# A new hand order for the attention part: row maxima product by product, transposes of v, mixer splits and a table load in other places

## The chip, the cores and the metric

One core of one Trainium2 chip runs the whole block as one program. The metric is device time in microseconds, lower is better; the kernel before took 1288.55 us (median of three runs, 1285.93 to 1289.34). The profile is one execution, taken by the hardware profiler. Five engines have an instruction queue each: TensorE (PE; its weight loads are listed as PEld), VectorE (DVE), ScalarE (ACT), GpSimd (POOL) and SyncE (SP, which here issues every DMA). Each queue is served in order.

## The reference, cut to what matters

A block of a streaming encoder over 16 meta tokens and 1024 frames, width 1024, all in float32. The mixer has four retention heads and eight forgetting-attention heads of width 64; the attention is

```
logits = einsum('bqhd,bkhd->bhqk', q, k) * dh**-0.5 + c_q - c_k      # c: running sum of log f
p      = softmax(where(causal & valid, logits, -1e30))
o_f    = einsum('bhqk,bkhd->bqhd', p, v)
h      = h + concat(o_r, o_f) @ w_out
h      = h + conv_ffn(rms_norm(h))
```

A final norm follows. The change touches only the order in which the attention and what lies around it are issued.

## The kernel before

Products that need float32 precision are made of three matmuls: each operand is split into a rounded high part and a low part (`split`, line 116: ACT writes the high part, another engine subtracts), and high by high, high by low and low by high are summed in a PSUM bank.

After the retention heads comes the attention part, some 185 to 560 us of the span. Its order on TensorE, DVE, ACT and POOL is written out by hand (`tc.manual_schedule`): what the program emits first runs first on each engine. Two streams are woven together.

The dense stream is the generator `dense()` (line 632). It goes through units of 96 matmuls, each giving one 128-wide slice of a projection: fq, fk, fv (queries, keys, values of a pair of heads) and rg (a retention gate); the last one is fv3. Each unit has four chunks (24 matmuls of some 256 columns), each evicted by DVE (L672, L674) from the two banks psD. It yields 120 budget units a matmul, and `run(upto)` draws from it until the budget `done` reaches `upto`. A unit is thus U = 11,520. Side work is put in a list `late` and popped after so many matmuls ("ticks"): `v_tiles` (line 602) transposes a chunk of v into the one bank psT (L606), from which ACT and DVE write high and low parts (L611, L612); in fv3, also splits of mixer tiles 0 to 3 (`split_m`, line 872). What is left at the end of fv3 is flushed with a yield of 400 each. Then `fill` (line 884) does the output projection's first six of eight mixer tiles for six output slices (L894, 160 units a matmul of 342 columns); before the tiles 4 and 5 are used for the first time, they are split. They are loaded while fv3 runs.

The attention stream goes through eight heads with 13 steps each (`units`; a step is at most 512 columns of logits in one psS bank, and there are three of these). A step t draws half of its dense share, issues its logits (`part_s`: L787, mask L791; ACT exponentiates, L797, and rounds, L799), the low part of the step before (`part_d`, L805), other work by the step's number in its head (`at`), the other half of the dense share (`run(want)`), and the value products of three steps ago (`part_v`, L824). The budget `GOAL` gives a head some 21,900 units, a step 1,685, half a step 842, which is seven matmuls.

The maxima of a head's logits are needed before its first step, so they are built a head ahead. `max_step(h, j)` (line 721) takes the queries of row tile j against all keys up to it, 512 columns to a product: one product for j = 0 to 3, two for 4 to 7, three for 8, 15 in all. Each product takes a psS bank (L730, its last one with a mask, L732), and DVE reduces it (L733). `max_end` combines them (L738 to L741). `max_rows` (line 744) transposes the result in psT (L747), ACT copies it (L749), and SP writes it to DRAM (`md`, L750) and reads it back into two rows of `qB` (L752, L753), which the head's logits use. Today row tiles go to steps by

```
SPLIT = (4, 4, 5, 5, 6, 7, 8, 8, 9)     # row tile j -> step of the head before
```

so the steps 4 to 9 issue 2, 2, 2, 2, 4 and 3 products, all at once; `max_end` comes at step 9, `max_rows` at step 10 ahead of the second half of the dense share. Head 0's products are woven into the unit fv0 by lines of their own, a row tile after every 768 units. `prep_k` and `prep_q` (lines 697, 712) make a head's operands: two ACT copies, two DVE subtractions, DMAs for the second copies. `norm2` (step 10) applies the softmax sums.

When all is done, the rest of the output projection starts (`rest_mm` L1069; DVE adds the residual, L1081; ACT squares it, L1093 and L1104). Behind its first slice a dummy square root (`warm`, L1419) makes ACT load the table of that function, which later norms use.

Of the kernel before, what the change touches and what calls it, by code (L numbers as in the profile page):

```python
# [12 lines left out]
AF = mybir.ActivationFunctionType  # L13
# [4 lines left out]
P = 128  # L18
NM = 16
NF = 1024  # L20
NT = NM + NF
# [60 lines left out]
def tile_hymba_block(ctx, tc, xt, xn, wrv0, wrv1, wft, wout, wup, wdn, small, cst, rope, dtab, out):  # L82
# [549 lines left out]
    def dense():  # L632
        late, c = [], 0

        def add(*x):
            nonlocal c
            if not late:
                c = 0
            late.extend(x)

        def tick():
            nonlocal c
            c += 1
            if late and c >= late[0][0]:
                late.pop(0)[1]()
                c = 0

        for u, nm in enumerate(units_w):
            kind, i_ = nm[:2], int(nm[2])
            if kind == "wo":  # L650
                break
            w_dma(u + 1)
            chunks = CX_Q if kind in ("fq", "rg") else CX_T
            t0 = Q0 if kind in ("fq", "rg") else 0
            if kind in ("fq", "fk"):
                st = fq.tile([P, NT], F32, tag=kind, name=kind)
                (qst if kind == "fq" else kst)[i_] = st
            else:
                st = stage("vst" if kind == "fv" else "gate")
                st = st[:, :NQ] if kind == "rg" else st  # L660
            for ci, (a, n) in enumerate(chunks):
                ps = bank(pj)
                for k in range(KT):
                    w_h, w_l = (t[:, k % 4, :] for t in wts[u][k // 4])
                    for i, (w_, e) in enumerate(((w_h, 0), (w_h, 1), (w_l, 0))):
                        pe.matmul(ps[:, :n], lhsT=w_, rhs=X(e, k, t0 + a, n),  # L666
                                  start=(k == 0 and i == 0), stop=(k == KT - 1 and i == 2))
                        yield 120
                        tick()
                rbs = rb[:, t0 + a:t0 + a + n]  # L670
                if kind == "fq":
                    dve.scalar_tensor_tensor(st[:, t0 + a:t0 + a + n], ps[:, :n], 0.125, rbs, op0=ALU.mult, op1=ALU.mult)  # L672
                else:
                    dve.tensor_tensor(st[:, a:a + n], ps[:, :n], rbs, op=ALU.mult)  # L674
                if ci == 1:
                    w_split(u + 1)
                if kind == "fv":
                    add((16, lambda st=st, i_=i_, g=VT[ci]: v_tiles(st, i_, *g)))
                if nm == "fv3":
                    for k in (2 * ci, 2 * ci + 1):  # L680
                        mt[k] = xbuf(ci, f"m{k}")[:, :2 * NQ].rearrange("p (i n) -> p i n", i=2)
                        if k < NA:
                            load_m(k, mt[k])
                    if ci in (1, 2):
                        add(*[(8, lambda k=k: split_m(k)) for k in (2 * ci - 2, 2 * ci - 1)])
            if kind == "rg":
                add(*[(14, g) for g in gate_tail(i_, st)])
        for _, g in late:
            yield 400
            g()  # L690
        wb_done[0] = True
        yield from fill(units_w.index("wo0"))
# [25 lines left out]
        dve.tensor_tensor(qB[s][h_, c], qst[p][h_, c], f(q1[s])[h_, c], op=ALU.subtract)  # L718
        dup[0] = sp.dma_start(f(q1[s])[o_, c], f(q1[s])[h_, c])

    def max_step(h, j):
        s = h % 2
        t0, R = KTILES[j]
        q_ = Q0 if j == 0 else 0
        w = min(NT, P * j + P)
        for ci, a in enumerate(range(0, w, 512)):
            n = min(512, w - a)
            last = a + n == w
            ps = bank(pS)
            pe.matmul(ps[:R - q_, :n], lhsT=qm[s][:, t0 + q_:t0 + R], rhs=kB[s][:, a:a + n], start=True, stop=not last)  # L730
            if last:
                pe.matmul(ps[:R - q_, n - R:n], lhsT=msk[:, q_:R], rhs=idr[:, :R], start=False, stop=True)  # L732
            dve.tensor_reduce(mxs[s][:R - q_, j, ci:ci + 1], ps[:R - q_, :n], axis=mybir.AxisListType.X, op=ALU.max)  # L733
# [150 lines left out]
    def fill(u0):  # L884
        pss = {}

        def part(d, ci, ks, first, stop):
            if first:
                pss[ci] = bank(pj)
            ps, (a, n) = pss[ci], CH_Q[ci]  # L890
            for k in ks:
                w_h, w_l = (t[:, k % 4, :] for t in wts[u0 + d][k // 4])
                for i, (w_, hl) in enumerate(((w_h, 0), (w_h, 1), (w_l, 0))):
                    pe.matmul(ps[:, :n], lhsT=w_, rhs=mt[k][:, hl, a:a + n],  # L894
                              start=(first and k == ks[0] and i == 0), stop=(stop and k == ks[-1] and i == 2))
                    yield 160
            if stop:
                dve.tensor_tensor(hst[d][:, a:a + n], ps[:, :n], hst[d][:, a:a + n], op=ALU.add)

        h_load(0)  # L900
        w_dma(u0 + 1)
        for d in range(EARLY):
            h_load(d + 1)
            if d == 0:
                yield from part(d, 0, range(4), True, False)
                yield from part(d, 1, range(4), True, False)
                split_m(4)
                split_m(5)
                yield from part(d, 0, range(4, 6), False, True)
                yield from part(d, 1, range(4, 6), False, True)  # L910
            else:
                yield from part(d, 0, range(6), True, True)
                w_split(u0 + d + 1)
                w_dma(u0 + d + 2)
                yield from part(d, 1, range(6), True, True)
            if d == 0:
                w_split(u0 + d + 1)
                w_dma(u0 + d + 2)
            yield from part(d, 2, range(6), True, True)
            sp.dma_start(hres[d], hst[d])  # L920
        w_split(u0 + EARLY + 1)
# [6 lines left out]
    done = [0]  # L928
# [9 lines left out]
    V = U  # L938
# [5 lines left out]
        GOAL[h] = max(GOAL[h], u * U + 1)  # L944
    for h, u in ((2, 7), (4, 11)):
        GOAL[h] = min(GOAL[h], u * U)
    SPLIT = (4, 4, 5, 5, 6, 7, 8, 8, 9)
    with tc.manual_schedule(engines=ENG):
        for s_ in range(2):
            rs_ = fp.tile([P, NQ], F32, tag="o", name="rss", bufs=2)  # L950
# [8 lines left out]
            max_step(0, j)  # L959
        run(2 * U + V * 14 // 15)  # L960
        m2 = max_end(0)
        prep_k(1)
        prep_q(1)
        run(2 * U + V + 1 + U // 8)
        max_rows(0, m2)
        scale_rows(1, lambda n: fp.tile([P, NQ], F32, tag="o", name=n, bufs=2))
        run(GOAL[0])
        for h in range(2, 4):
# [1 line left out]
        for t in range(len(units) + LAG):  # L970
            h, at = divmod(t, NU)
            if h < 7:
                want = GOAL[h] + (GOAL[h + 1] - GOAL[h]) * (at + 1) // NU
            else:
                want = GOAL[7] + (END - GOAL[7]) * (t - 7 * NU + 1) // (NU + LAG)
            run((done[0] + want) // 2)
            if h == 6 and at == 4:
                fqs.close()
                wA[0] = mk(fqs, "wA", side="right")
            if h == 6 and at == 4:  # L980
                m7 += [mt[7][:, 0, :], mt[7][:, 1, :]]
            if h == 6 and at == 12:
                load_m(6, mt[6])
                w6r = mk(wb, "w6r")
                for d in range(4):
                    wo_raw[d] = w6r.tile([P, (KT - NA) * P], F32, name=f"wo_raw{d}")
                    sp.dma_start(wo_raw[d], wout[d][:, NA * P:])
            if h == 7 and at == 4:
                split_m(6)
            if t < len(units):  # L990
                part_s(t)
            if 0 <= t - 1 < len(units):
                part_d(t - 1)
            if 0 < h and at == 6:
                norm1(h - 1)
            if 0 < h and at == 10:
                norm2(h - 1)
            if t < len(units):
                if h < 7:
                    if at == 0 and h > 0:  # L1000
                        prep_q(h + 1)
                    if at == 1 and h > 0:
                        prep_k(h + 1)
                    for j in range(9):
                        if SPLIT[j] == at:
                            max_step(h + 1, j)
                    if at == SPLIT[8]:
                        m2 = max_end(h + 1)
                    if at == SPLIT[8] + 1:
                        max_rows(h + 1, m2)  # L1010
            run(want)
            if t - LAG >= 0:
                part_v(t - LAG)
        run(1 << 50)
# [378 lines left out]
    with tc.manual_schedule(engines=ENG):  # L1393
# [20 lines left out]
        for di, d in enumerate(ORD):  # L1414
            r = mm(0, di)
            if di < 4:
                split_w(di + 2)
                if di == 0:
                    act.activation(warm, epsc, AF.Sqrt)  # L1419
            rest_h(0, d, r)  # L1420
            rest_acc(0, rest_sq(0, d), dve if di == 7 else pool)
            if di == 1:
# [486 lines left out]
```

## Time and profile before

| | |
|---|---|
| median of three runs | 1288.55 us (1285.93 to 1289.34) |
| the profiled execution, its own time | 1289.05 us |
| its span, from first to last instruction | 1287.2 us |
| TensorE matmuls busy | 1253.1 us, 97% |
| weight loads | 1189.2 us, 92% |
| DVE | 910.1 us, 71% |
| ACT | 588.8 us, 46% |
| POOL | 348.7 us, 27% |
| mean granted clock of TensorE | 0.991 |

A busy time is the time in which at least one instruction of the engine ran. Weight loads run beside matmuls. In rows of single instructions the columns are start and duration in us, engine, line, operation, tiles (written<-read), shape and count; in brackets the idle time before it and what ended it. A wait names the engine and line that waits, and the one whose signal came last.

### The profile page before, as it was taken

The page shows a single profiled execution, that of the slowest core. Times are in us where ns is not written, and L with a number is a line of the kernel's source. Part 1 is how long each engine was busy: PE and PEld are TensorE (multiplying, and loading weights), DVE is VectorE, ACT ScalarE, POOL GpSimd, SP SyncE. Part 2 cuts the span into 40 slices and gives each one's busy share as a digit, 9 for nine tenths or more (in the row PEclk, how much of TensorE's full clock was granted, in tenths as well). Part 3 has the DMA queues.
Part 4 walks back from the last instruction along what each step waited for, and adds up shares of the span by engine and source line. Part 5 has one row for each costly group of instructions (what it writes and reads, how often), then busy time and mean ns, then how long its engine had stood idle before and what let it go on. Part 6 is the DMA issues. An engine that isn't in the chain of part 4 may idle for free.

```text
span 1287.2 us, 24215 instructions
## 1 busy us (share of the span) xinstructions
PE 1253.1 (97%) x9279; PEld 1189.2 (92%) x9279; DVE 910.1 (71%) x1568; ACT 588.8 (46%) x1174; POOL 348.7 (27%) x294
## 2 busy tenths in 40 slices
PE   8999999999999989999899999999999999999997
PEld 8899999999999989988899999999999998888886
DVE  5776545556665576658987887879889887585664
ACT  7663441456355444445443343333433335544453
POOL 0154244000000000012254554645546450140001
PEclk9999999999999999999999999999999999999998
DMA  8533114213224435364154534537565579866652
GB/s 292 174 88 105 36 51 115 69 43 79 81 62 112 123 108 166 100 222 135 58 192 128 180 118 154 162 114 227 169 215 188 181 231 348 296 212 199 192 167 99
DMA packets 110965, 192.78 MB, mean 150 GB/s; under 512 B 15160, under 2 KB 50312, under 8 KB 110849
## 3 DMA queue, kind: packets, MB, share of 16 engines
q1 hardware_dynamic: 110848, 191.23, 47.0%
q8 instruction: 73, 1.20, 0.4%
q14 instruction: 44, 0.35, 0.1%
HBM read 132.59 MB, written 52.21 MB: 144 GB/s over the span
## 4 chain that ended last, share of the span: by engine, by line
PE 82%; DVE 6%; issue 4%; DMA 3%; ACT 3%; POOL 1%; SPq 0%; POOLq 0%; DVEq 0%; ACTq 0%
PE psb L1232 13%; PE psD L666 12%; PE psc L1232 9%; PE psa L1232 9%; PE psO L824 4%; PE psD L894 4%; PE psb L1388 3%; PE psx L1388 3%; PE psa L1388 3%; PE psc L1388 3%; PE psS L787 3%; PE psj L183 2%; PE psj L185 2%; PE psj L184 2%; PE psS L730 2%
## 5 line engine op out<-in xcount | busy, mean ns | idle before, releaser
L1198 DVE TENSOR_TENSOR d_u<-d_raw,d_u 128x512 fp32r<-128x512 f32 x154 | 110.0, 760 | 53.6 <-ACT d_u L1197 53.4
L1197 ACT CAST d_u<-d_raw 128x512 fp32r<-128x512 f32 x154 | 88.4, 619 | 92.3 <-PE psc L1388 35.3
L666 PE MATMUL psD<-xl,f_hi 128*128 128x256 f32 (+2 forms) x448 | 129.9, 290 | 0.0
L666 PE MATMUL psD<-xh,f_hi 128*128 128x256 f32 (+2 forms) x448 | 128.9, 288 | 0.4 <-DVE fq L672 0.4
L666 PE MATMUL psD<-xh,f_lo 128*128 128x256 f32 (+2 forms) x448 | 128.8, 288 | 0.0
L1193 POOL TENSOR_TENSOR S<-u_raw 128x512 f32<-128x512 f32 x42 | 59.7, 1420 | 203.0 <-DVE unit L1211 169.0
L1232 PE MATMUL psb<-B0T,unit 128*128 128x256 f32 x780 | 104.0, 282 | 1.6 <-DVE unit L1211 0.9
L1232 PE MATMUL psb<-B1T,unit 128*128 128x256 f32 x780 | 103.4, 281 | 1.3 <-ACT B1T L1158 1.2
L797 ACT ACTIVATE pf<-psS 128x272 f32<-128x272 f32 (+4 forms) x112 | 49.7, 451 | 113.8 <-PE psS L787 69.9
L1232 PEld LDWEIGHTS psb<-B0T,unit 128*128 128x128 f32 x780 | 97.2, 189 | 2.2 <-DVE unit L1211 1.4
L1232 PEld LDWEIGHTS psb<-B1T,unit 128*128 128x128 f32 x780 | 97.1, 189 | 1.7 <-ACT B1T L1158 1.5
L666 PEld LDWEIGHTS psD<-xh,f_hi 128*128 128x128 f32 x448 | 85.4, 191 | 0.9 <-DVE fq L672 0.6
L666 PEld LDWEIGHTS psD<-xl,f_hi 128*128 128x128 f32 x448 | 85.2, 190 | 0.4
L666 PEld LDWEIGHTS psD<-xh,f_lo 128*128 128x128 f32 x448 | 85.2, 190 | 0.1
L1211 DVE TENSOR_TENSOR unit<-S,unit 128x512 fp32r<-128x512 f32 x87 | 78.7, 906 | 4.2 <-ACT unit L1207 3.9
L1394 POOL MEMSET on<- 128x128 f32 x1 | 0.2, 204 | 296.5 <-PE psS L791 296.5
L733 DVE TENSOR_REDUCE mx<-psS 128x1 f32<-128x512 f32 (+6 forms) x120 | 59.0, 539 | 30.2 <-PE psS L730 20.9
L1207 ACT CAST unit<-S 128x512 fp32r<-128x512 f32 x87 | 54.1, 622 | 54.1 <-POOL S L1193 53.4
L183 PE MATMUL psj<-rv_hi,xh 128*128 128x256 f32 (+1 forms) x264 | 76.1, 292 | 1.7 <-DVE z L287 1.1
L1271 ACT ACTIVATE ca<-at,sm 128x1024 f32<-128x1024 f32 x22 | 25.3, 1152 | 110.0 <-DVE at L1263 110.0
L184 PE MATMUL psj<-rv_lo,xh 128*128 128x256 f32 (+1 forms) x264 | 75.5, 288 | 0.1
L185 PE MATMUL psj<-rv_hi,xl 128*128 128x256 f32 (+1 forms) x264 | 75.3, 288 | 0.0
(350 smaller groups left out, 3567.1 us busy)
## 6 DMA issues: line engine op xcount, KB each, us to landing
u_raw<-wup SPq DMA_DIRECT2D x44, 512.0 KB
sd<-wdn SPq DMA_DIRECT2D x88, 128.0 KB
uB<-u SPq DMA_DIRECT2D x44, 256.0 KB
wS<-sd SPq DMA_DIRECT2D x88, 128.0 KB
d_raw<-wS SPq DMA_DIRECT2D x44, 256.0 KB
d_raw<-uT SPq DMA_DIRECT2D x44, 256.0 KB
d_raw<-wdn SPq DMA_DIRECT2D x33, 256.0 KB
d_raw<-uB SPq DMA_DIRECT2D x33, 256.0 KB
```

The source lines that it names most:

```text
L183: pe.matmul(ps[:, :w], lhsT=x_h, rhs=w_h[:, c0:c0 + w], start=(k == 0), stop=False)
L184: pe.matmul(ps[:, :w], lhsT=x_h, rhs=w_l[:, c0:c0 + w], start=False, stop=False)
L185: pe.matmul(ps[:, :w], lhsT=x_l, rhs=w_h[:, c0:c0 + w], start=False, stop=(k == KT - 1))
L666: pe.matmul(ps[:, :n], lhsT=w_, rhs=X(e, k, t0 + a, n), start=(k == 0 and i == 0), stop=(k == KT - 1 and i == 2))
L733: dve.tensor_reduce(mxs[s][:R - q_, j, ci:ci + 1], ps[:R - q_, :n], axis=mybir.AxisListType.X, op=ALU.max)
L1193: (eng or pool).tensor_tensor(t, s_[x], s_[y], op=o)
L1197: act.copy(t[:, 0], src)
L1198: eng.tensor_tensor(t[:, 1], src, f(t[:, 0]), op=ALU.subtract)
L1207: act.copy(t[:, 0], srcs[ft][nm])
L1211: dve.tensor_tensor(t[:, 1], srcs[ft][SEQ[i][0]], f(t[:, 0]), op=ALU.subtract)
L1232: pe.matmul(ps[:, :n], lhsT=w[:, wi, k * P:(k + 1) * P], rhs=o[:, hl, k, :], start=(new and j == 0), stop=(j == 11), skip_group_check=not new)
L1388: pe.matmul(ps[:, c:c + n], lhsT=a_[:, wi, j * P:(j + 1) * P], rhs=b_[:, hl, c:c + n], start=(new and m == 0), stop=(kt == KH - 1 and m == ...
```

## The change

The same instructions are issued in another order; none is added or taken away.

- `max_step` can issue one product alone. In the main loop the 15 products go to the steps 4 to 9 as 3, 3, 2, 2, 2 and 3, and between two of a step an equal part of the second half of its dense share is drawn. `max_end` stays at step 9, behind the last product.
- `max_rows` at step 10 comes behind the second half of the dense share instead of ahead of it.
- For head 0, `max_rows` comes at the end of fv0 (2U + V + 1, with V = U), and head 1's `prep_k` and `prep_q` behind it, U/8 later; before, they came right behind `max_end`, and `max_rows` was last.
- The transposes of v are popped after 22 matmuls instead of 16. In fv3 this moves the splits of tiles 0 and 1 by six matmuls, and the third group of transposes to the flush, which has four groups with a yield of 400 instead of three.
- In `fill`, tile 4 is split ahead of the first 12 matmuls, tile 5 ahead of the second 12, instead of both behind the 24.
- The dummy square root comes behind the last exponentials (step index `len(units)`), instead of into the rest of the projection.

```diff
@@ dense
                 if kind == "fv":
-                    add((16, lambda st=st, i_=i_, g=VT[ci]: v_tiles(st, i_, *g)))
+                    add((22, lambda st=st, i_=i_, g=VT[ci]: v_tiles(st, i_, *g)))
@@ max_step
-    def max_step(h, j):
+    def max_step(h, j, only=None):
...
         for ci, a in enumerate(range(0, w, 512)):
+            if only not in (None, ci):
+                continue
@@ fill
             if d == 0:
+                split_m(4)
                 yield from part(d, 0, range(4), True, False)
+                split_m(5)
                 yield from part(d, 1, range(4), True, False)
-                split_m(4)
-                split_m(5)
@@ main loop of the attention part
-    SPLIT = (4, 4, 5, 5, 6, 7, 8, 8, 9)
+    MAXS = [(j, ci) for j in range(9) for ci in range((min(NT, P * j + P) + 511) // 512)]
+    SPLIT = {4: 3, 5: 3, 6: 2, 7: 2, 8: 2, 9: 3}
...
         m2 = max_end(0)
+        run(2 * U + V + 1)
+        max_rows(0, m2)
+        run(2 * U + V + 1 + U // 8)
         prep_k(1)
         prep_q(1)
-        run(2 * U + V + 1 + U // 8)
-        max_rows(0, m2)
...
+            if t == len(units):
+                act.activation(warm, epsc, AF.Sqrt)
...
-                    for j in range(9):
-                        if SPLIT[j] == at:
-                            max_step(h + 1, j)
-                    if at == SPLIT[8]:
+                    if at in SPLIT:
+                        lo = sum(v for k, v in SPLIT.items() if k < at)
+                        n_ = SPLIT[at]
+                        b0_ = done[0]
+                        for x in range(n_):
+                            max_step(h + 1, *MAXS[lo + x])
+                            if x < n_ - 1:
+                                run(b0_ + max(0, want - b0_) * (x + 1) // n_)
+                    if at == 9:
                         m2 = max_end(h + 1)
-                    if at == SPLIT[8] + 1:
-                        max_rows(h + 1, m2)
             run(want)
+            if h < 7 and at == 10:
+                max_rows(h + 1, m2)
@@ rest of the output projection
                 split_w(di + 2)
-                if di == 0:
-                    act.activation(warm, epsc, AF.Sqrt)
```

## The prediction

> **What bounds the kernel now.** I read the page first, then busy times by stretch, then the waits of the weight loader in the attention part, then single instructions in order of time at each place that the change touches.
>
> ```profile
> PE 1253.1 (97%) x9279; PEld 1189.2 (92%) x9279; DVE 910.1 (71%) x1568; ACT 588.8 (46%) x1174; POOL 348.7 (27%) x294
> ```
>
> TensorE is busy 97% of the span. The change takes no matmul away, so all it can gain is time in which TensorE stands. The page hides part of that, because ends of matmuls are modelled; the idle time of the weight loader PEld, and the distance between two matmuls' starts, show it better. By stretch (start:end, length, then busy time of PE, PEld, DVE, ACT and POOL with counts, PE clock, DMA share, GB/s), the first row being the attention part:
>
> ```profile
> 233.00:560.00 327.00, 320.46 (x2475) 308.00 (x2474) 199.86 (x396) 163.03 (x338) 0.20 (x1) 0.99 0.34 98
> ...
> 460.00:464.00 4.00, 3.28 (x21) 2.68 (x19) 3.68 (x9) 1.78 (x5) 0.00 (x0) 1.00 0.46 146
> ...
> 468.00:472.00 4.00, 2.07 (x11) 1.29 (x11) 3.73 (x8) 2.09 (x3) 0.00 (x0) 1.00 0.00 0
> 472.00:476.00 4.00, 4.00 (x17) 3.92 (x18) 2.99 (x5) 1.80 (x5) 0.00 (x0) 0.57 0.17 21
> ```
>
> DVE is at 61% of the part (199.86 of 327) and ACT at 50%, so on average neither bounds it; but DVE is full from 460 to 472, and there PE stands most. What PEld waited for in the part (total, times, longest):
>
> ```profile
> PEld psS L730 <- ACT pf L797: 6.1, 14, 0.7
> PEld psS L730 <- DVE mx L733: 2.6, 7, 0.6
> PEld psD L894 <- DVE m L118: 1.6, 2, 1.4
> PEld psT L606 <- DVE vst L674: 1.4, 2, 1.0
> ...
> PEld psD L894 <- ACT m L117: 1.1, 1, 1.1
> PEld psT L606 <- issue: 0.8, 1, 0.8
> ...
> PEld psS L787 <- DMA qB<-md: 0.4, 1, 0.4
> ```
>
> All but the last sit at instructions that the change moves: products for row maxima (L730), mixer splits (L117, L118, read by L894), transposes of v (L606). What follows TensorE's attention work is again TensorE's, so a microsecond won there should stay won.
>
> **The products.** Nothing is added. Today a step issues up to four products in a row, while psS has three banks of which the step's logits hold one. The pace of an undisturbed stream from the chain of waits, then one head's step 8 (two rows of two products) and step 9:
>
> ```profile
> 230.18 4.75 PE psD L666 x40
> ```
>
> ```profile
> 257.90 0.57 PE L730 MATMUL psS<-kB,qm 128*128 128x512 f32 x2
> ...
> 258.55 1.03 PE L730 MATMUL psS<-kB,qm 128*128 128x512 f32 x2
> 259.42 0.22 PE L732 MATMUL psS<-idr,msk 128*128 128x128 f32 x1
> ...
> 262.12 0.83 PE L730 MATMUL psS<-kB,qm 128*16 128x512 f32 x3
> 262.81 0.17 PE L732 MATMUL psS<-idr,msk 128*16 128x16 f32 x1
> ```
>
> 4.75 us over 40 matmuls of some 256 columns is 0.119 each, 0.463 ns a column. Step 8 streams 896 + 1024 columns and one mask product of 128: 0.95 us; from 257.90 to 259.42 it took 1.52, a loss of 0.57. Step 9 streams 1040 columns, 0.48, and took 0.69: 0.21. That is 0.78 a head and 5.5 over the seven heads whose maxima are built in the main loop. With a product at a time, and two or more dense matmuls behind each, a bank has time to be read out. Two ends: all 8.7 us of PEld's waits at L730 go; or as many stay as where head 0's maxima are already spread among dense matmuls, 0.8 us for its 15 products:
>
> ```profile
> PE psT L606 <- DVE vst L674: 1.7, 1, 1.7
> ...
> PEld psS L730 <- DVE mx L733: 0.8, 2, 0.4
> ```
>
> Seven times 0.8 stay then, and 8.7 - 5.6 = 3.1 is won. I take 5.0, near the start-to-start reading, with 0.5 left as waits.
>
> **v later.** In that stretch (213 to 233) the first row above is a stand of 1.7 for the last transposes of fv0. DVE had two subtractions of head 1's preparation in front of the eviction that they need; the second is the last row here:
>
> ```profile
> 224.66 0.38 PE L606 MATMUL psT<-idf,vst 128*128 128x128 f32 x2
> 225.48 0.42 DVE L612 TENSOR_TENSOR vaL<-psT,vaH 128x256 fp32r<-128x256 f32 x1 [0.20 <-ACT vaH L611]
> 227.83 1.22 DVE L718 TENSOR_TENSOR qB<-fq,q 64x1026 fp32r<-64x1026 f32 x1
> ```
>
> The preparation now comes behind the maxima of head 0, so this wait goes. But psT is one bank, held from 224.66 to 225.90, 1.24 us, by one group of transposes. The third group now pops two matmuls ahead of the chunk's end, and the transpose of the maxima is issued three matmuls (0.36 us) behind it: a new stand of about 0.9. Head 1's own loads, with their ACT, DVE and SP work, come 2,209 budget units (18 matmuls, 2.2 us) later and are wanted only at step 4 of head 0. So -0.8 there. In fv1 to fv3 six matmuls (0.7 us) more cover the longest waits, 1.0 and 0.8, nearly: -1.6 of 2.2. Together -2.4; ends -3.9 and 0 (the waits come back as psT or stage buffers held longer). The four idle entries at fv3's end become five groups in a changed order, without PE work of their own: nothing.
>
> **The splits.** TensorE stood for tiles 4 and 5 here; the loads had been issued long before (last row), and DMA is idle by 468:
>
> ```profile
> 469.19 0.42 PE L894 MATMUL psD<-m,f_hi 128*128 128x342 f32 x1 [0.77 <-ACT m L117]
> 470.75 0.42 PE L894 MATMUL psD<-m,f_hi 128*128 128x342 f32 x1 [1.13 <-DVE m L118]
> ```
>
> ```profile
> 469.48 2.36 DVE L118 TENSOR_TENSOR m<-m 128x1026 fp32r<-128x1026 f32 x2
> ```
>
> ```profile
> 450.48 1.16 SPq L870 DMA_DIRECT2D m<-mixg  x2
> ```
>
> A stand of 0.8 + 1.1 to 1.1 + 1.4; I take 2.3. Right after it the granted clock is 0.57 for 4 us: 1.7 us more. Issued 24 and 12 matmuls earlier both stands go, and with them I expect the clock's fall. [...]
> Against it: 2.36 us of DVE work enter 458 to 464, where DVE is at 3.68 of 4.00, ahead of product evictions and logit remainders. Between 0 and 2.36 of it shows; I take 0.8, as the remainders are wanted three steps later. And the path of the maxima below gives back 1.3 of the clock's 1.7. So -4.0 + 0.8 + 1.3 = -1.9; ends -4.0 and +0.4.
>
> **Maxima to rows later.** The transposes, the copy and three DMAs move behind the step's second half of dense work: 842 units, seven matmuls, 0.84 us; the step's own maxima end later too, but a whole step ahead. Head 6, whose rows came late, and head 7, the tightest of the others (SP's and PE's instructions):
>
> ```profile
> 475.99 0.46 SPq L750 DMA_DIRECT2D md<-mr  x1
> ...
> 480.30 0.25 SPq L752 DMA_DIRECT2D qB<-md  x1
> ```
>
> ```profile
> 482.20 0.35 PE L787 MATMUL psS<-qB,kB 128*128 128x242 f32 x1 [0.19 <-DMA qB<-md]
> ```
>
> ```profile
> 514.37 0.27 PE L747 MATMUL psT<-idf,m 128*18 128x128 f32 x1
> ```
>
> ```profile
> 515.60 0.29 SPq L750 DMA_DIRECT2D md<-mr  x1
> ...
> 518.62 0.24 SPq L753 DMA_DIRECT2D qB<-md  x1
> ```
>
> ```profile
> 521.66 0.28 PE L787 MATMUL psS<-qB,kB 128*128 128x242 f32 x1
> ```
>
> Head 6's second read was issued 0.3 behind 480.30 and landed by 482.20: 1.6. With 1.6, head 7 has 521.66 - 520.2 = 1.4 to spare, more than 0.84: cost 0 in all heads but 6. In head 6 SP is held by an earlier DMA that waits for the normalization on DVE, so 0.84 vanishes in that; but if PE no longer loses 1.7 us to the clock, it arrives earlier and waits for the same DMAs: the 1.3 charged above (ends 0 and 2).
>
> **The table load.** It sat ahead of a square whose input was ready at 565.07 + 0.43 = 565.50:
>
> ```profile
> 564.58 1.28 ACT L1419 ACT_TABLE_LOAD   x1
> ```
>
> ```profile
> 565.07 0.43 DVE L1081 TENSOR_TENSOR Hp<-psa,Hp 128x258 f32<-128x258 f32 x1
> ```
>
> ```profile
> 565.98 0.40 ACT L1093 ACTIVATE acc<-Hp 128x258 f32<-128x258 f32 x1
> ```
>
> So 0.5, not 1.5, comes off the relay of ACT and DVE that TensorE then waits on. Moved behind the last exponential it lies in ACT's idle time before the last head's outputs (11.5 us in four waits; uncovered it would cost 1.5):
>
> ```profile
> ACT m L836 <- DVE o L835: 11.5, 4, 3.3
> ```
>
> ```profile
> 567.00:571.00 4.00, 2.06 (x14) 1.55 (x12) 2.44 (x6) 1.43 (x4) 1.38 (x2) 1.00 0.98 322
> 571.00:575.00 4.00, 3.59 (x18) 3.62 (x19) 1.79 (x6) 1.89 (x5) 2.77 (x4) 0.57 0.89 300
> ```
>
> The relay itself stays, and so I leave the clock's fall at 571 in. -0.5; ends 0 and -2.2 (the fall, 1.7, goes too).
>
> **The sum.** -5.0 - 2.4 - 1.9 + 0 - 0.5 = -9.8. The profiled execution took 1289.05 us by its own time (span 1287.2 and 1.85 around it), 0.5 above the median of 1288.55; 1289.05 - 9.8 is 1279.2, and 1278.8 from the median. I say 1279.
>
> **The rivals.** (a) DVE gives half of it back: the waits stay with a product's eviction queued behind splits, evictions and normalizations. Products then give 3.1, v and splits nothing, the load 0.5 and the spread-out preparation 0.8: -4.4, 1284.5. For it: DVE at 3.7 of 4.00 around 460 to 472; against it: 61% elsewhere.
> (b) The rows come late in every head. If each write to DRAM took the 4.3 us of head 6 (475.99 to 480.30) instead of head 7's 2.7 (515.60 to the first read, 0.3 ahead of 518.62), 1.6 more, then 1.6 + 0.84 - 1.4 = 1.0 a head, 6 to 7 in all: -3, 1286. Against it: the one wait of 0.4 in eight heads.
> (c) Slower: an evicted product now lies later in the step, so the next step's logits (L787) find no psS bank. It decides from 14 us, 0.33 in each of 42 product steps (six in each of seven heads): the 9.8 are eaten and 4 are lost, 1293. For it: the last product has only a third of half a share behind it; against it: 0.8 us of such waits in all of head 0's spread products.
> (d) The order does not matter: the stands at products are taken up by later ones, since dense work is only moved within a step: 1288.5. Against it: the chain goes through TensorE and nothing else is near full.
>
> **Chances.** The forecast (1273 to 1283) 0.60, (a) 0.18, (b) 0.09, (c) 0.06, (d) 0.07. About 0.3%, 3.9 us, is what a measurement of this kernel can tell from no change. Faster by more: the forecast, two thirds of (a), half of (b): 0.77. Within: the rest of those and (d), 0.16. Slower: (c) and a little, 0.07. The lower end takes products at 8.7 and the clock's falls with them, 1272; the upper reaches over (b) to 1287.
>
> **What would show it.** Right: PEld's waits at L730 fall from 8.7 to under 2 in the part; no stand at the mixer products around 469, and no fall of the clock right behind it; L606 under 1; a new psT wait of about 0.9 at head 0's maxima; waits for the maxima's rows only at head 6, 1 to 2 us; the square starts when its input is ready. Wrong: waits of L787 for L733 or for the DMA of the maxima in most heads, new waits for DVE between 458 and 468, or a clock that falls in new places.

## The result, and the profile after

The changed kernel takes 1277.72 us (median of 18 runs, 1275.41 to 1288.34), the kernel before, run beside it, 1286.39 (18 runs). The medians lie 8.7 apart; the ratio over all runs is 0.9939, interval 0.9925 to 0.9954, which is 7.8 us less (5.9 to 9.6). The forecast was 1279, 9.8 below the profiled execution of before. That is near in the sum; most terms were not. In part the nearness is luck: over 18 runs the kernel before is 2.2 faster than the median of three that the forecast started from, and that hides a gain forecast 1 to 2 us too large.

The execution that was profiled took 1287.03 us by its own time (span 1285.3), the second longest of the 18: near 205 and 220 us a pair of subtractions on DVE took 5.64 and 3.00 instead of 1.28, beside work of GpSimd that the change does not touch (last section), and the clock fell at 224 (0.57 from 224 to 228). So the first row of the table below cannot be compared (with v alone it is 17.11); the stages behind it can.

The page of the changed kernel:

```profile
PE 1251.4 (97%) x9279; PEld 1192.7 (93%) x9279; DVE 917.8 (71%) x1568; ACT 589.3 (46%) x1174; POOL 350.3 (27%) x294
```

Busy time hardly moved. Between starts of matmuls it did (us; each stage runs from the first matmul of the product named to the next):

| stage | before | after |
|---|---|---|
| fv0, where head 0's maxima are built | 16.27 | 19.99 |
| fq1 to the first logits of head 0 | 8.94 | 7.90 |
| first logits of head 0 to last logits of head 7 | 316.86 | 308.35 |
| to the last product with v | 8.06 | 8.79 |
| to the first w6 product of the last head | 4.32 | 5.39 |
| to the sum of squares of the norm | 12.48 | 12.07 |

The third row, the main loop, carries the gain: 8.5 us. The fall of the granted clock at 472, which before had, is not in it any more; it lasted 3.41 us at half speed, some 1.7 us of loss, as did the falls in the loops below. Beside it the loop is 6.8 shorter. The two rows below it give back 1.8.

Busy times by stretch of the changed kernel (columns as before):

```profile
237.00:556.00 319.00, 314.84 (x2479) 308.25 (x2478) 201.08 (x399) 165.05 (x343) 0.20 (x1) 1.00 0.35 101
...
465.00:470.00 5.00, 4.22 (x28) 3.80 (x29) 4.53 (x7) 3.29 (x7) 0.00 (x0) 1.00 0.01 2
470.00:475.00 5.00, 3.91 (x27) 3.49 (x26) 4.90 (x13) 1.90 (x5) 0.00 (x0) 1.00 0.11 13
```

The clock stays at 1.00, but TensorE still stands at 465 to 475, where DVE is at 4.5 and 4.9 of 5. What PEld waits for in the part after:

```profile
PEld psS L732 <- ACT pf L799: 2.2, 3, 1.2
PEld psD L896 <- DVE hst L900: 1.6, 2, 1.3
PEld psT L606 <- DVE vaL L612: 0.8, 1, 0.8
PEld psT L749 <- DVE m L743: 0.7, 2, 0.6
PEld psS L732 <- DVE mx L735: 0.7, 2, 0.5
PEld psD L666 <- DVE fq L672: 0.6, 1, 0.6
```

The products' waits (L730 before, L732 now) went from 8.7 us in 21 to 2.9 in 5. The waits for the splits (L118, L117: 1.6 and 1.1) and for vst (L674: 1.4) are gone. In their place stands the row of vaL. The row of L896 for hst, fill's own eviction on DVE, was there before with one wait of 1.1, at 543:

```profile
PEld psD L894 <- DVE hst L898: 1.1, 1, 1.1
```

Now that one is 0.3, and a new one of 1.3 stands at 474.

### The profile page after: what moved, and what is told of

Read it like the earlier page. It is cut to its first block, busy times and chain, and to the rows that moved or that the text cites. A ratio compares the mean times of both kernels' runs of the same rounds, so it can differ in the third digit from the quotient of the medians.

```text
span 1285.3 us, 24208 instructions
## 1 busy us (share of the span) xinstructions
PE 1251.4 (97%) x9279; PEld 1192.7 (93%) x9279; DVE 917.8 (71%) x1568; ACT 589.3 (46%) x1174; POOL 350.3 (27%) x294
## 4 chain that ended last, share of the span: by engine, by line
PE 83%; DVE 7%; issue 3%; ACT 3%; DMA 3%; POOL 1%; SPq 0%; POOLq 0%; DVEq 0%; ACTq 0%
PE psb L1243 13%; PE psD L666 11%; PE psc L1243 9%; PE psa L1243 9%; PE psO L826 4%; PE psD L896 4%; PE psb L1399 3%; PE psx L1399 3%; PE psa L1399 3%; PE psc L1399 3%; PE psS L789 3%; PE psj L183 2%; PE psj L185 2%; PE psj L184 2%; PE psS L732 1%
## 5 line engine op out<-in xcount | busy, mean ns | idle before, releaser
L735 DVE TENSOR_REDUCE mx<-psS 128x1 f32<-128x512 f32 (+6 forms) x120 | 61.7, 541 | 29.5 <-PE psS L732 16.7
```

## The experiments

Main loop means the third row of the table. Each profile is one execution; a loop with a clock fall in it is told with the fall.

**Products alone.** The kernel before with `max_step(h, j, only)`, MAXS and the new SPLIT; `max_rows` stays ahead of the second half of step 10:

```
-                    for j in range(9):
-                        if SPLIT[j] == at:
-                            max_step(h + 1, j)
+                    if at in SPLIT:
...
+                            max_step(h + 1, *MAXS[lo + x])
+                            if x < n_ - 1:
+                                run(b0_ + max(0, want - b0_) * (x + 1) // n_)
```

> The kernel before with the products alone spread (3, 3, 2, 2, 2, 3 by step, dense work between them); everything else as before, the maxima's rows included. Theory (the stands at psS banks go and stay gone): 4.5 to 6 us faster, ratio about 0.996; PEld's waits at the product line fall from 8.7 to under 2 us over the attention part, and each of heads 0 to 6 becomes 0.6 to 0.9 us shorter. Rival (the evictions on DVE hold the banks anyway): 0 to 3 us, with PEld still waiting 5 us or more there. Second rival (won in the attention part, given back behind it, because the end of that part hangs on DMA and DVE): heads shorter by 5 us in sum, yet the first matmul of the up projection less than 4 us earlier.

1281.55 us, ratio 0.9978 (0.9960 to 0.9996), so 2.8 us (0.5 to 5.1); the medians lie 4.6 apart, and the times alone do not rule out 5. The trace says less: the loop took 313.10 without a fall, 2.1 less than before without its fall (315.2). Its PEld waits, largest first:

```profile
PEld psT L749 <- DVE m L743: 2.2, 2, 1.4
PEld psD L896 <- ACT m L117: 1.6, 1, 1.6
PEld psS L732 <- ACT pf L799: 1.4, 2, 0.7
PEld psT L606 <- DVE vst L674: 1.4, 2, 1.0
PEld psD L896 <- DVE m L118: 1.2, 2, 0.9
```

The waits at products went, and a new one leads: the transpose of the maxima (L749) waits for the end of their own calculation (L743). The last product now comes a third of a half share later, so `max_end` is late for a `max_rows` that has not moved. Heads 0 to 3 were each 0.57 to 0.75 shorter, near the 0.78 forecast, and head 6 was 1.1 shorter. Head 4 was 1.5 longer, and head 5 gained nothing beside the fall.

**Rows alone**, and **products with rows**: `max_rows` behind `run(want)` in the kernel before, and both edits.

```
-                    if at == SPLIT[8] + 1:
-                        max_rows(h + 1, m2)
             run(want)
+            if h < 7 and at == 10:
+                max_rows(h + 1, m2)
```

> The kernel before with only the maxima's rows behind the second half of step 10's dense share. Prediction: no cost but at head 6, where SP is held by another DMA: 0 us, at most 1 slower. Rival (b) of the prediction: 0.5 to 1 us a head, 4 to 7 us slower, with waits of the logits for the DMA into qB in most heads.

> The kernel before with the products spread and the maxima's rows behind the second half of step 10: the two together. With the products alone, one head lost 1.5 us, since the transpose of the maxima (at the start of step 10) then stood 1.36 us for reductions that the spreading makes later. Theory (the move of the rows is what the spreading needs, it has no gain of its own): that head's loss goes, heads 0 to 6 are 5.5 to 7 us shorter in sum than before against 3.8 with the products alone. Rival (the two are independent, so the sum of the two single runs): 3.5 to 4.5 us, the transpose still waiting over 1 us.

Rows alone: 1285.84 us, ratio 1.0009 (0.9991 to 1.0026), no change. Together: 1281.94, ratio 0.9980 (0.9965 to 0.9994). The loop is 313.34 with a clock fall at 463 in it, so 3.6 less than before beside the falls, against 2.1 for the products alone; the wait at L749 fell to one of 0.5. The times can't tell 2.1 from 3.6. Heads 0 to 6 are 3.5 shorter, where my theory had 5.5 to 7. What is left of the maxima's loss is now at head 6 (PE, then SP's queue):

```profile
475.34 0.35 PE L789 MATMUL psS<-qB,kB 128*128 128x242 f32 x1 [1.07 <-DMA qB<-md]
```

```profile
467.90 0.36 SPq L884 DMA_DIRECT2D hst<-xt  x1
468.30 0.87 SPq L864 DMA_DIRECT2D mixg<-o  x1
469.26 0.46 SPq L752 DMA_DIRECT2D md<-mr  x1
469.81 1.19 SPq L544 DMA_DIRECT2D f_raw<-wout  x2
473.48 0.25 SPq L754 DMA_DIRECT2D qB<-md  x1
```

The write of the maxima stands behind a load of 513 KB (hst) and a store of 256 KB (mixg), with more loads behind it (f_raw), and 4.2 us pass from its issue to the first read's.

**Splits alone.** In the kernel before:

```
+                split_m(4)
                 yield from part(d, 0, range(4), True, False)
+                split_m(5)
                 yield from part(d, 1, range(4), True, False)
-                split_m(4)
-                split_m(5)
```

> The kernel before with only the splits of mixer tiles 4 and 5 moved ahead of the first and second 12 matmuls. Prediction's step: both stands at 468 to 471 us (2.3 us) and the clock's fall behind them (1.7 us) go, DVE's extra load costs 0.8 and the wait for the maxima's rows of head 6 grows by 1.3: 1.9 us faster. Theory after the first result: the rows of head 6 do not wait at all, since the normalization ahead of them no longer stands behind the splits on DVE, but DVE's extra load shows as 2 to 3 us of stands at products and transposes between 455 and 473: again 1.5 to 2.5 us faster, with the terms otherwise shared out. Rival: without the spread products DVE's queue costs as much as the stands, 0 us.

1284.40 us, ratio 0.9989 (0.9975 to 1.0002). The loop was 315.00: 1.9 less, as forecast, and nearly all of it is the clock, which did not fall at 472. The stands went from the mixer products to the neighbours, and the rows of head 6, which by my theory were not to wait at all, came 0.9 late. PEld between 440 and 490:

```profile
PEld psS L730 <- DVE mx L733: 1.5, 2, 0.8
PEld psS L730 <- ACT pf L797: 1.3, 2, 0.7
PEld psT L606 <- DVE vst L674: 1.0, 1, 1.0
PEld psS L787 <- ACT pf L797: 1.0, 1, 1.0
PEld psS L787 <- DMA qB<-md: 0.9, 1, 0.9
```

**v alone**, with head 0's order:

```
-                    add((16, lambda st=st, i_=i_, g=VT[ci]: v_tiles(st, i_, *g)))
+                    add((22, lambda st=st, i_=i_, g=VT[ci]: v_tiles(st, i_, *g)))
...
+        run(2 * U + V + 1)
+        max_rows(0, m2)
+        run(2 * U + V + 1 + U // 8)
         prep_k(1)
         prep_q(1)
-        run(2 * U + V + 1 + U // 8)
-        max_rows(0, m2)
```

> The kernel before with the transposes of v after 22 matmuls and head 0's maxima ahead of head 1's preparation. Prediction: 2.4 us faster: the stand of 1.7 us at head 0's last transposes goes, a new one of 0.9 for the one psT bank comes at the maxima's transpose; in fv1 to fv3 1.6 of 2.2 us go. Rival: the waits only move (the bank psT, DVE's eviction of the next chunk): 0 to 1 us faster.

1285.63 us, ratio 0.9998 (0.9985 to 1.0011): nothing. The loop was 1.2 shorter beside the fall (314.02 without one), but the stretch to the last product with v 0.73 longer and that to the first w6 product 1.35.

**The table load alone** (the `warm` square root at `t == len(units)`), timed once:

> The kernel before with only the table load moved. Prediction: the square of the first slice starts when its input is ready, 0.4 to 0.5 us sooner counted from the last value product, and all later work with it; the clock's fall in that stage stays, the load costs nothing at its new place. Rival (the load delays ACT's exponentials or copies at the new place): the last value product or the last head's outputs come 0.5 to 1.5 us later.

1286.25 us. From the first w6 product to the norm 10.95 us, against 11.38 in executions of the old order whose clock did not fall there: 0.43.

**The changed kernel with the splits put back** behind the 24 matmuls:

> The changed kernel with the two mixer splits of tiles 4 and 5 put back behind the 24 dense matmuls of step 0; products, rows, transposes of v and table load stay as changed. Theory: the splits' move is worth more inside the change than alone. The stands at the mixer products come back (about 1.3 and 0.9 us near 465 to 470), head 6's logits wait again about 1.2 us for the DMA of their maxima, because the normalization is held behind the splits on DVE, and the granted clock falls behind the stand in some executions (1.7 us). Main loop from head 0's first to head 7's last logits 2.5 to 5 us longer than the changed kernel's 308.35 (about 311 to 313), median 1280.5 to 1283. Rival (the terms simply add): 1 to 2 us longer, 309.5 to 310.5, no wait at head 6's logits.

1280.57 us, ratio 0.9958 (0.9938 to 0.9977), beside 0.9939: 2.4 slower, with intervals that overlap. The loop was 310.34, 2.0 longer than 308.35, the clock's fall included. PE and the clock there:

```profile
470.25 0.42 PE L896 MATMUL psD<-m,f_hi 128*128 128x342 f32 x1 [1.13 <-DVE m L118]
471.39 0.43 PE L896 MATMUL psD<-m,f_hi 128*128 128x342 f32 x1 [0.40 <-DVE m L118]
```

```profile
472.00:476.00 4.00, 4.00 (x20) 3.85 (x19) 2.08 (x4) 1.90 (x5) 0.00 (x0) 0.61 0.53 122
```

The stands and the fall came back; the wait at head 6's logits, which my theory had, did not, which fits TensorE's coming late itself. By the median (1280.5 to 1283 was my theory's) the times cannot decide; the loop shows the rival's loss of 1 to 2. In this execution, too, the move of the splits is worth the clock's 1.7 and little more, and my theory of a larger worth has nothing in the trace to rest on.

**The changed kernel with v after 16 entries:**

> The changed kernel with the transposes of v again after 16 entries instead of 22; everything else, the order of head 0's preparation too, as changed. Theory: the later transposes only shift fill work behind the last logits. The stretch from the last logits to the last product with v goes back from 8.79 to about 8.06, the stretch to the first dense w6 matmul from 5.39 to about 4.4, and the main loop grows by about 1.2 (308.35 to about 309.5): net within 1 us of the changed kernel's 1277.7. Rival (the forecast of 1.6 for fv1 to fv3 stands): 1.6 us or more slower, 1279.3 and above, with waits of 0.8 to 1.0 us at the transposes of fv1 to fv3.

1277.75 us, ratio 0.9940 (0.9919 to 0.9962), the same as the changed kernel. The two stretches behind the loop went back to 8.06 and 4.58, as expected, and PEld's waits of 1.0 and 0.8 at the transposes of v are back. The loop was 311.55, 3.2 longer instead of 1.2, and 1.8 of it, counted between starts, is this (PE, then SP):

```profile
477.92 0.35 PE L789 MATMUL psS<-qB,kB 128*128 128x242 f32 x1 [1.63 <-DMA qB<-md]
```

```profile
470.77 0.27 SPq L752 DMA_DIRECT2D md<-mr  x1
471.14 0.36 SPq L884 DMA_DIRECT2D hst<-xt  x1
...
473.47 0.29 SPq L754 DMA_DIRECT2D qB<-md  x1
```

Against the 3.2 stand 1.5 in the two stretches behind the loop and 1.0 at head 0: fv0 and the next stretch take 16.34 and 7.71, 24.05 together, against 25.01 with v alone. That leaves a loss of 0.7 in this execution, too little for the times to show. So inside the change v's later transposes win in the loop about what they lose ahead of it and behind it.

**wo7's weights sooner.** The changed kernel, with the raw weights of the last output slice in a buffer of their own and loaded a slice sooner:

```
+                raw = wf.tile([P, 512], F32, tag="raw", name="f_raw", bufs=RB) if nm != "wo7" else \
+                    wA[0].tile([P, 512], F32, name=f"w7_{hf}")
...
-                w_dma(u0 + d + 2)
+                if d < EARLY - 1:
+                    w_dma(u0 + d + 2)
+                if d == EARLY - 2:
+                    w_dma(u0 + d + 3)
```

> The changed kernel with one more edit: the weights of the last output slice (wo7) get a raw buffer of their own and are loaded about 9 us sooner, ahead of the residual's loads. Theory (the attention part's end hangs on this load: ACT's and DVE's split of it stands ahead of the last head's reciprocal on DVE, so 1.8 us of the gain are given back there): the split is done before the last value product, the reciprocal starts within 0.3 us of it, and the kernel is 1.5 to 2 us faster than the changed one, ratio to before 0.992 to 0.9925. Rival (the end hangs on the last value products and the residual's loads): under 0.5 us.

1278.74 us, ratio 0.9943 (0.9929 to 0.9958): by the times no gain. In the trace the step is there: last product with v to first w6 product 4.20 instead of 5.39. In the changed kernel the reciprocal of the last head stands behind the late weights' subtractions; here it comes at 550.38, right behind subtractions that no longer wait. DVE, the changed kernel first:

```profile
557.63 1.31 DVE L118 TENSOR_TENSOR f_lo<-f_raw,f_hi 128x512 fp32r<-128x512 f32 x2 [1.07 <-ACT f_hi L117]
558.97 1.85 DVE L836 RECIPROCAL o<-psO 64x272 f32<-64x272 f32 x1
```

```profile
549.07 1.28 DVE L118 TENSOR_TENSOR f_lo<-w,f_hi 128x512 fp32r<-128x512 f32 x2
550.38 1.85 DVE L837 RECIPROCAL o<-psO 64x272 f32<-64x272 f32 x1
```

**Without GpSimd's long sums.** The changed kernel; the sums over partitions of retention heads 2 and 3 are left out, and a constant takes their place:

```
-            head_sum(2 + s_, rs_, sqs[s_], slice(0, NQ))
+            pool.memset(rs_, 128.0)
+            sp.dma_start(ro_d[2 + s_][:, slice(0, NQ)], rs_[0:1, :])
```

> The changed kernel without the two sums over partitions on GpSimd for retention heads 2 and 3 (a constant stands in their place, so these heads are scaled wrongly); it is there to show what these sums do to others. Theory: a DVE subtraction that runs beside them takes up to 5 us instead of 0.68, in some executions, and TensorE stands behind it; without them the split at about 205 us takes 0.7 us a half, the runs of over 1280 us go, and the mean falls by 1 to 2.5 us against the changed kernel's 1279.1. Rival (the stands come from late weight loads): the spread and the mean stay.

1278.10 us, ratio 0.9944 (0.9930 to 0.9957). The median does not move, and the mean falls by 1.0 (1278.2 against 1279.1), where 1 to 2.5 was expected; what it shows of DVE is in the last section.

**Two subtractions on GpSimd.** The kernel with wo7 sooner, and the low parts of the splits of tiles 4 and 5 on POOL:

```
-        split(m[:, 0, :], m[:, 1, :], f(m)[:, 1, :], dve)
+        split(m[:, 0, :], m[:, 1, :], f(m)[:, 1, :], pool if k in (4, 5) else dve)
```

> The changed kernel with wo7's weights loaded sooner (as in e_tail) and the low parts of the mixer splits of tiles 4 and 5 taken on GpSimd instead of VectorE. Theory: what is left to lose between 455 and 473 us is VectorE's crowding (stands of 0.74, 0.77, 0.44, 1.05 and 1.25 in the changed kernel); without 4.7 us of subtractions there, 2 to 3 us of these stands go, median 1275.5 to 1277. Rival: GpSimd's own tensor operation (2.4 us or more each, two a tile) slows VectorE's subtractions beside it (2.4 instead of 0.68 us) and comes late for the mixer products: no gain or 1 to 3 us slower, 1278 to 1281, with stands at the mixer products for m on POOL.

1277.38 us, ratio 0.9931 (0.9909 to 0.9953), not to be told from the changed kernel. The stands of 1.05 and 1.25 at 465 and 473 shrank to 0.60 and to nothing: DVE's crowding had caused most of them. But the gain meets the next wait, with the DMA engines busy ahead of it:

```profile
465.00:470.00 5.00, 5.00 (x39) 4.96 (x38) 2.62 (x6) 2.56 (x7) 0.00 (x0) 1.00 0.79 236
```

```profile
472.24 0.35 PE L790 MATMUL psS<-qB,kB 128*128 128x242 f32 x1 [1.06 <-DMA qB<-md]
```

**Head 6's rows through GpSimd's queue**, on top of that:

```
+        rq = pool if h == 6 else sp
-        sp.dma_start(md[s].rearrange("i (j p) -> (i j) p", p=P), mr)
+        rq.dma_start(md[s].rearrange("i (j p) -> (i j) p", p=P), mr)
```

> The kernel e_mpool with one more edit: the three small DMAs that carry head 6's maxima to rows of qB (one write of 9 KB, two reads) are issued by GpSimd, which is idle there, instead of SyncE, where they stand behind loads of 513 and 256 KB and two loads of f_raw. Theory: where VectorE is no longer the hold-up, head 6's logits wait for these rows because the loads are ahead of the write and of the reads (e_mpool: write issued at 465.56, 0.6 us after the copy, first read issued only at 470.36, PE standing 1.23 us until 472.24). Issued by GpSimd the write starts at about 465.0 and the rows land before 471: the 1.23 us of head 6 go, main loop 307.7 to about 306.4, median 1276.0 to 1276.5. Rival: the DMA engines are the limit (0.79 busy between 465 and 470), or GpSimd's own issue is slow; then the rows come no sooner, the wait stays at 1 to 2 us, and the time stays within 0.5 us of e_mpool's 1277.4 or above it.

1280.63 us, ratio 0.9948 (0.9923 to 0.9973): no gain, and the wait is longer, 3.10 instead of 1.06 (POOL, then PE):

```profile
462.18 0.85 POOL L754 DMA_DIRECT2D md<-mr  x1 [2.71 <-ACT mr L752]
467.78 0.51 POOL L756 DMA_DIRECT2D qB<-md  x1 [4.75 <-DMA md<-mr]
```

```profile
471.18 0.35 PE L791 MATMUL psS<-qB,kB 128*128 128x242 f32 x1 [3.10 <-DMA qB<-md]
```

The write no longer stands behind anything on its own queue, and 4.75 us still pass before the first read can be issued; hst and mixg had been issued 0.7 and 0.3 us ahead of it, by SyncE at 461.49 and 461.90. My theory, that the place in SyncE's queue was the cause, is not borne out; that GpSimd's issue is slow by itself, the rival's second half, no run excludes. What fits the runs is the order of issue: the rows are late where the small write, or the read, goes out behind large transfers, by whichever queue. No run moves these transfers, so this is read from the traces, not shown.

## Why the prediction came out near, point by point

**Bound and place: right.** TensorE's stands were the only thing to gain. The waits at products fell to 2.9 us in the part (under 2 was forecast), there is no fall behind 469, and no waits of L787 came in their place: rivals (b), (c) and (d) are out. Of rival (a) the place is right, DVE between 455 and 475, the size is not.

**Products: mis-sized, 5.0 forecast, 2.1 alone and 3.6 with the rows.** The 0.78 a head nearly held in heads 0 to 3. In heads 4 to 6 other waits took most of it: alone, that of the transpose of the maxima in head 4 (1.4); with the rows, that of head 6 for its rows (1.23 between starts). The step that failed was to multiply by seven.

**Rows: forecast 0 as a cost, which "rows alone" bears out; as a part of the change it was wrong.** I wrote that the maxima end "a whole step ahead" without asking where that leaves the old place. The products alone lost up to 1.4 us at L749; with the rows moved, the loop is 1.5 shorter than with products alone.

**v: forecast 2.4, not found.** At head 0 the new stand came as forecast, 0.57 of idle time in this row of PE, 0.73 between starts (0.9 forecast):

```profile
232.66 0.28 PE L749 MATMUL psT<-idf,m 128*18 128x128 f32 x1 [0.57 <-DVE vaL L612]
```

With v alone fv0 is 0.84 longer and the next stretch 1.04 shorter: 0.2, not 0.8. "v after 16" tells the two edits apart: with head 0's order alone the two stretches are 1.16 shorter than before, and the later transposes take 0.96 of that back, at L749 and in fv0, where PEld waits 1.5 for evictions of products instead of 0.8. In the loop, 1.2 came of 1.6, and not all of it from the transposes: heads 0 to 5 gave 1.0 beside the fall, head 6 lost 0.5 to its rows, and 0.6 came in head 7, where fill no longer waits 0.8 for hst (30.1 us in all seven kernels with 16 entries, 29.5 in all seven with 22).

What failed besides is "five groups in a changed order, without PE work of their own: nothing". They are three entries that become four, with a yield of 400 each, and the work that this moves counts: between the last logits and the last product with v stand 24 products of fill and 23 of the rest of the projection instead of 22 and 19 (0.73 longer), and wo7's weights, issued at 551.09 behind the loads of Hp, come late for it (PE):

```profile
557.65 0.51 PE L1080 MATMUL psb<-m,f_hi 128*128 128x258 f32 x2 [0.24 <-ACT f_hi L117]
558.38 0.39 PE L1080 MATMUL psb<-m,f_lo 128*128 128x258 f32 x1 [0.22 <-DVE f_lo L118]
```

The first w6 product is 1.07 later for it, counted from the last product with v. Together that takes the 1.4 back.

**Splits: 1.9 forecast; 1.9 alone and 2.0 inside the change, in the loop.** The terms of the sum were in part others. Stands and clock went, about 4. Back came not 0.8 of crowding and 1.3 at head 6's rows but 1.05 and 1.25 of crowding and no row wait (DVE, PE and SP of the changed kernel):

```profile
460.55 2.37 DVE L118 TENSOR_TENSOR m<-m 128x1026 fp32r<-128x1026 f32 x2 [0.17 <-ACT m L117]
```

```profile
465.78 0.50 PE L732 MATMUL psS<-kB,qm 128*128 128x512 f32 x1 [0.89 <-ACT pf L799]
...
474.06 0.58 PE L896 MATMUL psD<-m,f_hi 128*128 128x342 f32 x2 [1.09 <-DVE hst L900]
```

```profile
472.75 0.26 SPq L752 DMA_DIRECT2D md<-mr  x1
...
475.01 0.72 SPq L755 DMA_DIRECT2D qB<-md  x1
```

Here the rows' write went out ahead of the loads, and TensorE, late for DVE's sake, reads them only at 480.03. Where it is not late, the forecast's 1.3 comes, more or less: 1.23 in "products with rows" and "two subtractions on GpSimd", 1.79 in "v after 16", 0.8 in "splits alone", all between starts. Taking the one wait away uncovers the other.

**The clock.** With the splits behind the 24 matmuls it fell between 463 and 474 in 5 of 7 profiled kernels, with them ahead and no row wait over 1.8 us in none of 6, and it fell again (471.7) behind the stand of 3.27 us between starts in the last experiment. With the splits put back it fell behind stands of 1.40 and 0.56 us; behind 1.26 and 0.97 in "products alone", and behind 1.79 in "v after 16", it did not. So in these runs neither the longest stand nor the sum of them tells whether the clock falls, and no run was made to show what does. The fall at 570 stayed (0.75 from 567 to 571, 0.82 from 571 to 575), and is in some of the profiles and not in others (1.1 us: 12.48 to the sum of squares with it, 11.38 without).

**The table load: right**, 0.4 of 0.5. It lies in ACT's idle time, and the square comes right behind Hp (ACT, then DVE):

```profile
550.56 1.28 ACT L1003 ACT_TABLE_LOAD   x1
...
563.76 0.42 ACT L1104 ACTIVATE acc<-Hp 128x258 f32<-128x258 f32 x1 [0.97 <-DVE Hp L1092]
```

```profile
563.30 0.43 DVE L1092 TENSOR_TENSOR Hp<-psa,Hp 128x258 f32<-128x258 f32 x1
```

**The sum.** By the stages: 6.8 and 1.7 in the loop, 0.4 at the table load, 0.2 at head 0 (from "v alone"), less 1.8 behind the loop: 7.3, against 7.8 timed. In the loop the edits alone, beside falls, give 2.1, 0.3 (rows), 0.2 and 1.2, which is 3.8 of 6.8. That they help one another is seen for products and rows (3.6 against 2.4). The rest, 1.8 us, lies at head 6: it is 0.5 longer than before with splits alone and with v alone and 0.2 longer with products and rows, as it waits for its rows in each of them, and 1.1 shorter in the changed kernel, which has no such wait. With the splits put back it is 1.1 shorter, too. Each of these is one execution, and no edit was made to show the reason.

## What to carry to other kernels

Multiply a stand's saving by its repeats only after asking, in each repeat, what waits next: here, with products and rows moved, four heads gave 3.3 of the 3.6 us, and three passed theirs on to other waits. A work item that makes its result later needs its consumer moved with it; measured apart, the one edit looks weak and the other useless. An idle-looking entry in a hand order still draws fill work through its budget, and what slides behind the last logits was lost there. Two edits that are measured as one can hide each other, as head 0's order and the later transposes did.

## What the runs showed of the hardware that was not expected

Beside GpSimd's long sums DVE's subtractions took longer in some executions, by very different amounts. DVE and POOL in the changed kernel, then DVE without the sums:

```profile
200.30 4.79 DVE L718 TENSOR_TENSOR qB<-fq,q 64x1026 fp32r<-64x1026 f32 x1 [1.12 <-ACT q L716]
...
205.70 5.64 DVE L118 TENSOR_TENSOR f_lo<-f_raw,f_hi 128x512 fp32r<-128x512 f32 x2
```

```profile
199.45 12.95 POOL L241 PARTITION_ALL_REDUCE rss<-rsq  x2 [6.29 <-issue]
```

```profile
195.63 1.22 DVE L718 TENSOR_TENSOR qB<-fq,q 64x1026 fp32r<-64x1026 f32 x1 [1.12 <-ACT q L716]
...
200.27 1.28 DVE L118 TENSOR_TENSOR f_lo<-f_raw,f_hi 128x512 fp32r<-128x512 f32 x2
```

1.22 became 4.79, and two of 0.64 became 5.64; in the kernel before, where the first of these subtractions ended just as the sums began, it took 1.22 and the two 2.27. Near 220, beside GpSimd's multiplication of 2.38, two subtractions took 3.00 in the changed kernel. In the kernel with wo7 sooner two subtractions wholly within the sums took no more than 2.15. What decides by how much they are slowed, no run was made to show. Of 18 runs of the changed kernel 5 lie above 1280 us, of 6 without the sums none: this is what one would see if the slowed subtractions made the long runs, but 6 are too few to show it.
